# Decoder block on one core: order of the closing steps in the input projection (rotary tiles, squares, second half)

## The chip, the cores and the metric

One core of one Trainium2 chip. The metric is the time on the device in microseconds (us) for one execution of the whole kernel, the median of several runs. TensorE (PE) multiplies matrices, VectorE (DVE) and ScalarE (ACT) work on tiles of 128 partitions, GpSimd (POOL) does a few element-wise steps; SyncE (SP), ScalarE and GpSimd issue DMA transfers in their own instruction queues. Every engine works through its queue in order.

## The reference

All of it is float32; S = 1024 tokens, D = 1024. What bears on the change is the first sub-layer:

```python
h = _rmsnorm(x, g_mix_pre[l])                      # x * rsqrt(mean(x*x) + EPS) * g
proj = einsum('bsd,de->bse', h, w_in[l]) + b_in[l]
u_pool, q, k, v, gates = split(proj, IN_SPLITS)    # 512, 512, 128, 128, 2048
q = _partial_rotary(q.reshape(B, S, 8, 64), cos, sin)   # first 16 of 64 channels
k = _partial_rotary(k.reshape(B, S, 2, 64), cos, sin)
y_attn = _sliding_window_sink_attention(q, k, v, sinks) # window 128, blocks of 128
```

Behind it follow a pooling mixer, sigmoid gates that merge both branches, an output projection, and an MLP with a squared ReLU, each with an RMS norm and a residual sum.

## The kernel before

The work is laid out with channels on partitions and tokens along the free dimension. Each float32 product is made of three matmuls on rounded operands: a value is split into a high part (a cast, mostly on ScalarE) and a low part (a subtraction, on VectorE), and `PASSES` multiplies high by high, high by low and low by high.

**Projection.** `w_qkv` gives six tiles of 128 channels, f = 0 to 5; the tokens come in two halves, th = 0 and 1, of 512. Tiles 4 and 5 hold the rotary rows of all heads (80 rows: queries 0 to 3 in rows 16m, keys in rows 64 to 79) and the remaining key rows; tiles 0 to 3 hold the remaining query rows and, in rows 48 to 79, the values. `mm_in(f, th, k)` issues the three matmuls of one k of eight. `scaled(k, th, ...)` (L200 to L203) multiplies x by the norm's gain into the high part on ScalarE and the low part on VectorE. The norm's row factor comes later: `square_row` sums the squares of the tokens, `factors(th)` takes the inverse square root (`rsqrt`, L109 to L121) and spreads it (L218), and `make_rb(th)` transposes it with four matmuls on TensorE (L224) and copies it to `rb` (L225).

`close_in(f, th)` multiplies a finished tile by `rb` on VectorE (L350) and adds the bias on ScalarE (L351). `turn` (L360) and `turn_end` (L364, L365) rotate the rotary rows: for the first half on VectorE, for the second half on GpSimd. Then small DMAs put rows in place: `keys_rest` (L376, L377, two moves), `rows_in` (L372, three moves for the keys and three for each of the four query tiles), `values_out` (L380, one per query tile). `split_k` and `split_q(n)` make high and low parts for the scores.

**Order.** In the first block only TensorE's order is as written; a planner sets the order of the other engines by data and its own costs. In the second block (from L941) the order of TensorE, VectorE and ScalarE is the written one; SyncE's and GpSimd's queues are set by the planner. After the first half's tiles come the squares of the second half's tokens (L949), the closes of tiles 4 and 5, the turn, and the closes of tiles 0 to 3, each followed by its `rows_in` on SyncE, ScalarE, ScalarE and GpSimd.

**The stream.** `others()` is a generator that yields groups of three matmuls: first the 48 groups of the second half (tiles 4, 5, 0, 1, 2, 3, eight k each), then the gates' products (`half`). `fill(t)` takes groups from it until t us of TensorE time (0.681 us per group) are issued, carrying the rest over in `owed`. When the last k of a tile is issued, the tile is closed at that place in the queues of VectorE and ScalarE, with its moves in SyncE's queue. Between the fills lie the attention steps of the eight blocks n: scores (`score_all`, L439 to L441), masks (`score_prev`, L448), maximum (L455), exponentials (L465), scaling (L471), transposes (`attend_t`, L482), products with the values (`attend_v`, L507) and the transposes of the values (`post_v`, L403). The operands of the gates are prepared by callbacks in `between`, flushed inside `half`, or at f = 3, k = 3 for the first of them.

PSUM has four rotating banks with the tag `mm`, for the second half's tiles, `make_rb`, `post_v` and the gates. SBUF tiles of one tag rotate too: three of tag `st` hold weights that come from memory.

Of the kernel before, what the change touches and what calls it, by code (L numbers as in the profile page):

```python
# [17 lines left out]
NT = S // P  # L18
# [32 lines left out]
def block_kernel(ctx: ExitStack, tc, xt, x, consts, vecs, sinks, rot, g_post, g_mlp, g_mlp_post,  # L51
# [132 lines left out]
    def mm_in(f, th, k, a=0, b=512):  # L184

        for j, (wh, xh) in enumerate(PASSES):
            pe.matmul(b_in[f, th][:, a:b], w_in_of(f, k, wh), xs_[k][th][:, xh, a:b],  # L187
                      start=k == 0 and j == 0 and a == 0, stop=k == NK - 1 and j == 2)
# [11 lines left out]
    def scaled(k, th, xs, a=0, b=512):  # L200
        t, gk = xs_[k][th], vec[:, V_G + k:V_G + k + 1]
        act.activation(t[:, 0, a:b], xs[:, a:b], AF.Identity, scale=gk)
        dve.scalar_tensor_tensor(t[:, 1, a:b], xs[:, a:b], gk, f32(t[:, 0, a:b]), ALU.mult, ALU.subtract)  # L203
# [21 lines left out]
        act.copy(rb[:, th * 512:(th + 1) * 512], b)  # L225

    NR = 80
    squares_late, rows_of = {}, {}
    tables = {}

    def load_table(th):
# [3 lines left out]
    with tc.manual_schedule(engines={mybir.EngineType.PE}):  # L235
        for k in range(NK):
            if k % 2 == 0:
                xs = at("s4", 4, [S])
                wkv.append(ga_.tile([P, 2, 2, 256], F32R, tag="ga", name=nm("wkv")))
            xk = xs[:, k % 2 * 512:(k % 2 + 1) * 512]  # L240
            ws = stage([768]) if k else ws_first
            if k == 0:
                nc.sync.dma_start(vec, vecs)
                for a, b in ((0, 256), (256, 512)):
                    nc.sync.dma_start(xk[:, a:b], xt[k][:, a:b])
                nc.sync.dma_start(ws[:, 512:], w_qkv[k][:, 512:])
            else:
                nc.sync.dma_start(xk, xt[k][:, :512])
                nc.sync.dma_start(ws, w_qkv[k])
            xs_.append([xp.tile([P, 2, 512], F32R, tag="x", name=nm("x")) for _ in range(2)])  # L250
            q = wslot([2, 512]) if k < 6 else ga_.tile([P, 2, 512], F32R, tag="ga", name=nm("wq"))
            kv = wkv[-1]
            wq.append(q)
            if k == 0:
                split(q[:, 0, :], q[:, 1, :], ws[:, :512], first=dve)
                scaled(k, 0, xk, 0, 256)
                scaled(k, 0, xk, 256, 512)
            else:
                scaled(k, 0, xk)
                split(q[:, 0, :], q[:, 1, :], ws[:, :512])  # L260
            split(kv[:, 0, k % 2, :], kv[:, 1, k % 2, :], ws[:, 512:])
            if k == 0:
                for a in (0, 256):
                    for f in range(4):
                        mm_in(f, 0, k, a, a + 256)
            elif k < 6:
                for f in range(4):
                    mm_in(f, 0, k)
            if k < 6:
                for f in (4, 5):  # L270
                    mm_in(f, 0, k)
        for f in (4, 5, 0, 1):
            for k in (6, 7):
                mm_in(f, 0, k)
        nc.sync.dma_start(cst, consts)
        for n in range(4):
            square_row(n, at("qkv", 3, [S]) if n < 3 else at("s4", 4, [S]))
        load_table(0)
        factors(0)
        for k in range(NK):  # L280
            if k % 2 == 0:
                xs = flat(yy.tile([P, 2, 512], F32, tag="y", name=nm("xs")))
            nc.sync.dma_start(xs[:, k % 2 * 512:(k % 2 + 1) * 512], xt[k][:, 512:])
            scaled(k, 1, xs[:, k % 2 * 512:(k % 2 + 1) * 512])
        for n in range(4, NT):
            squares_late[n] = at("s8", 3, [2, 4, P]).rearrange("p a b k -> p (a b k)") if n < 7 else at("s4", 4, [S])
            nc.sync.dma_start(squares_late[n], x[n])
# [86 lines left out]
    def keys_rest(q, th):  # L374
        t = raw_k[th] = at("s4", 4, [2, 512])[:, 0, :]
        q.dma_start(t[:48], raw_r[th][NR:, 0, :])  # L376
        q.dma_start(t[NR:], raw_r[th][NR:, 1, :])  # L377
# [9 lines left out]
    def split_v(src, tag, bufs):  # L387

        t = at(tag, bufs, [6, HD], F32R)
        pool.memset(f32(t[:, ::5, :]), 0.0)  # L390
        split(t[:, 1::3, :], t[:, 2:4, :], src, pool, pool)
        return flat(t)
# [7 lines left out]
    def post_v(n):  # L400
        b = bank("mm")
        t = tv[:, n * P:(n + 1) * P]
        pe.transpose(b[:, :P], t, ident)  # L403
        act.copy(t, b[:, :P])
        vf, old = (tv[:, i * P:(i + 1) * P].rearrange("p (h d) -> p h d", d=HD) for i in (n, max(n - 1, 0)))
        vs[n] = split_v(vf, "v", 4)
        if n:
            dv = at("df", 1, [2, HD])
            pool.tensor_tensor(dv, vf, old, ALU.subtract)
            dvs[n] = split_v(dv, "dv", 3)  # L410

    scores = {}
    SCALE = HD ** -0.5
# [361 lines left out]
    def others():  # L775
        for f in (4, 5, 0, 1, 2, 3):
            b_in[f, 1] = bank("mm")
            for k in range(NK):
                mm_in(f, 1, k)
                if f == 3 and k == 3:  # L780
                    flush(between[0])
                    flush(between[1])
                if k == NK - 1:
                    close_in(f, 1)
                    if f == 5:
                        keys_rest(nc.sync, 1)
                        turn(1, pool)
                        turn_end(1, pool)
                        rows_in(nc.sync, 1, raw_k[1], 4)
                    elif f < 4:  # L790
                        values_out(nc.sync, 1, f)
                    if f in (1, 2, 3):
                        rows_in(nc.sync, 1, raw_of(f - 1, 1), f - 1)
                    if f == 1:
                        split_k(1)
                yield 3 * 0.227
            if f == 2:
                gt.load(2 * spilled[0])
                between[0].append(lambda: gt.operand(spilled[0], 1))
        gt.load(2 * spilled[1])  # L800
        steps = [(p, i) for p in spilled + (6, 7) for i in (1, 2)]
        for j, (p, i) in enumerate(steps[:16]):
            if j == 1:
                rows_in(nc.sync, 1, raw_of(3, 1), 3)
            if j == 0:
                between[0].append(lambda: gt.operand(*steps[1]))
                between[0].append(lambda: gt.operand(*steps[2]))
            between[0].append(lambda j=j: gt.operand(*steps[j + 3]))
            if i == 1:
                gt.load(2 * steps[j + 4][0])  # L810
            gi = 3 - j // 4
            if j in (0, 4, 9, 13):
                load_wb(gi)
            yield from half(p, i)
            if j % 4 == 3:
                flush(lazy)
                yield from wb_mm(gi)
# [125 lines left out]
    with tc.manual_schedule(engines={mybir.EngineType.PE, mybir.EngineType.DVE, mybir.EngineType.Activation}):  # L943
        make_rb(0)
        for f in (2, 3):
            for k in (6, 7):
                mm_in(f, 0, k)
        for n in range(4, NT):
            act.activation(squares_late[n], squares_late[n], AF.Square, accum_out=ssq[:, n:n + 1])  # L949
        close_in(4, 0)  # L950
        close_in(5, 0)
        turn(0, dve)
        keys_rest(nc.sync, 0)
        turn_end(0, dve)
        rows_in(nc.sync, 0, raw_k[0], 4)
        for m in range(4):
            close_in(m, 0)
            rows_in((nc.sync, nc.scalar, nc.scalar, nc.gpsimd)[m], 0, raw_of(m, 0), m)
        for m in range(4):
            values_out(nc.gpsimd, 0, m)  # L960
        load_table(1)
        factors(1)
        fill(4.0)
        make_rb(1)
        act.activation(warm, r1[:, :1], AF.Exp)
        fill(1.4)
        presum(0)
        presum(0)
        dve.tensor_scalar(nsnk, snk, -1.0, None, ALU.mult)
        split_k(0)  # L970
        fill(6.5)
        split_q(0)
        fill(1.6)
        score_all(0)
        act.activation(tv[:, :512], tv[:, :512], AF.Identity, bias=vec[:, V_BV:V_BV + 1])
        score_prev(0, 0)
# [22 lines left out]
        for n in range(NT):  # L999
# [5 lines left out]
            if n + 1 < NT:  # L1005
                early = 1.0 if n > 2 else 0.0
                softmax_exp(n + 1, range(4))
                fill(early)
                softmax_exp(n + 1, range(4, 8))
                softmax_scale(n + 1)  # L1010
                if n != 2:
                    flush(lazy)
                fill((5.0 if n == 1 else 4.4) - early)
                hurry[0] = True
                fill(1.4)
                hurry[0] = False
                if n + 2 < NT:
                    split_q(n + 2)
            else:
                fill(4.0)  # L1020
                split_gate(0, lambda: xp.tile([P, 2, 512], F32R, tag="x", name=nm("T")))
# [1486 lines left out]
```

## Time and profile before

| | |
|---|---|
| median of 3 runs | 1124.87 us (1122.95 to 1125.82) |
| the profiled execution's time | 1125.5 us |
| its span, first to last instruction | 1123.7 us |
| mean granted TensorE clock | 0.982 |
| instructions | 14805 |
| ScalarE busy | 647.4 us (58%) |
| GpSimd busy | 100.0 us (9%) |

The profile is one execution. Times in its views are microseconds from the first instruction. A group or timeline row names the line, the engine, the operation, the output and the inputs, the shape, the count and the duration; in brackets stands the idle time of the engine just ahead and what ended it. `PEld` is TensorE's weight load, which overlaps its matmuls; `ACTq` and `SPq` are the queues of ScalarE and SyncE issuing DMAs. The granted clock is the share of full speed that the throttle let TensorE have in a stretch. An L101 or L104 is the split into high and low part, wherever it is called from, so it is told apart by its tile (`qt` queries, `khi` and `klo` keys, `wh` weights).

### The profile page before, as it was taken

What the parts mean: (1) busy time and instruction counts of PE and PEld (TensorE: products, weight loads), DVE (VectorE), ACT (ScalarE), POOL (GpSimd) and SP (SyncE); (2) the same over time, 40 slices, a digit from 0 to 9 for tenths busy, and PEclk for the clock granted to TensorE, in tenths of its full rate; (3) what the DMA queues carried; (4) which work ended last, traced back from release to release, by engine and by line L of the source; (5) the groups of instructions that cost most, each with busy time, mean ns of one, the idle gap of its engine ahead of it and who ended that gap; (6) DMA issues with size and microseconds to landing.
All of it is one profiled execution on the core that took longest, in us unless ns stands there. A gap on an engine that the chain in (4) does not pass through costs nothing.

```text
span 1123.7 us, 14805 instructions
## 1 busy us (share of the span) xinstructions
PE 1086.7 (97%) x5247; PEld 908.9 (81%) x5247; DVE 904.2 (80%) x1300; ACT 647.4 (58%) x1084; POOL 100.0 (9%) x149
## 2 busy tenths in 40 slices
PE   9588899999999999999999999999999999999997
PEld 7466678788888888888888888888888899899886
DVE  5557599899978788778997967777665899889997
ACT  6536688746665425758676665655554375275553
POOL 0132143110010001200000000010100000000000
PEclk9879899999999999999999999999999999999999
DMA  8634677977986576763257755555698868549842
GB/s 290 225 90 123 198 188 186 313 232 247 307 246 217 172 231 167 171 241 131 71 177 284 272 199 215 197 192 202 237 397 291 270 221 288 169 146 317 310 155 75
DMA packets 107593, 243.29 MB, mean 217 GB/s; under 512 B 10656, under 2 KB 28320, under 8 KB 107520
## 3 DMA queue, kind: packets, MB, share of 16 engines
q1 hardware_dynamic: 87152, 192.48, 50.9%
q0 software_dynamic: 14336, 29.69, 11.0%
q10 hardware_dynamic: 6032, 20.19, 4.7%
q8 instruction: 41, 0.67, 0.2%
q14 instruction: 32, 0.26, 0.1%
HBM read 166.30 MB, written 73.40 MB: 213 GB/s over the span
## 4 chain that ended last, share of the span: by engine, by line
PE 84%; DVE 6%; ACT 4%; DMA 3%; issue 2%; ACTq 0%; SPq 0%; DVEq 0%
PE mm L626 24%; PE at L626 18%; PE at L2193 12%; PE mm L2193 5%; PE mm L1587 5%; PE at L2167 4%; PE mm L2167 4%; PE mm L537 3%; PE at L1587 2%; PE at L1315 2%; PE mm L187 1%; PE mm L1315 1%; PE mm L539 1%; ACT s L465 1%; PE sc L439 1%
## 5 line engine op out<-in xcount | busy, mean ns | idle before, releaser
L2193 PE MATMUL at<-ar,wh 128*128 128x512 f32 x564 | 134.6, 389 | 0.0
L2193 PEld LDWEIGHTS at<-ar,wh 128*128 128x128 f32 x564 | 105.8, 188 | 22.2 <-DVE ar L104 0.3
L104 DVE TENSOR_TENSOR wh<-st,wh 128x512 fp32r<-128x512 f32 (+1 forms) x106 | 77.9, 745 | 32.0 <-ACT wh L101 28.3
L101 ACT CAST wh<-raw 128x1024 fp32r<-128x1024 f32 (+1 forms) x54 | 53.4, 988 | 79.5 <-PE at L2193 52.0
L626 PE MATMUL mm<-T,wx 128*128 128x512 f32 x375 | 90.6, 389 | 0.0
L104 DVE TENSOR_TENSOR wh<-raw,wh 128x1024 fp32r<-128x1024 f32 (+1 forms) x54 | 61.7, 1143 | 29.7 <-ACT wh L101 29.2
L626 PEld LDWEIGHTS mm<-T,wx 128*128 128x128 f32 x375 | 70.3, 188 | 14.8 <-DVE wx L104 0.2
L101 ACT CAST wh<-st 128x512 fp32r<-128x512 f32 (+2 forms) x105 | 67.6, 653 | 19.7 <-DVE st L582 5.7
L626 PE MATMUL mm<-gr,wh 128*128 128x512 f32 x321 | 77.5, 391 | 0.0
L626 PEld LDWEIGHTS mm<-gr,wh 128*128 128x128 f32 x321 | 59.9, 188 | 12.2
L2193 PE MATMUL mm<-ar,wh 128*128 128x512 f32 x276 | 69.5, 389 | 0.0
L626 PE MATMUL mm<-T,wh 128*128 128x512 f32 x267 | 66.0, 389 | 0.0
L626 PE MATMUL mm<-x,wh 128*128 128x512 f32 x240 | 60.2, 401 | 3.9 <-ACT wh L101 3.9
L101 ACT CAST ar<-B 128x1024 fp32r<-128x1024 f32 (+2 forms) x59 | 43.0, 757 | 30.7 <-PE mm L2193 14.8
L2193 PEld LDWEIGHTS mm<-ar,wh 128*128 128x128 f32 x276 | 51.8, 188 | 10.8
L626 PE MATMUL at<-gr,wh 128*128 128x512 f32 x243 | 59.0, 389 | 0.0
L626 PEld LDWEIGHTS mm<-T,wh 128*128 128x128 f32 x267 | 50.1, 188 | 10.4
L626 PEld LDWEIGHTS mm<-x,wh 128*128 128x128 f32 x240 | 45.0, 191 | 14.1 <-ACT wh L101 4.4
L626 PEld LDWEIGHTS at<-gr,wh 128*128 128x128 f32 x243 | 45.6, 188 | 9.5
L626 PE MATMUL at<-T,wx 128*128 128x512 f32 x213 | 52.2, 389 | 0.0
L104 DVE TENSOR_TENSOR ar<-B,ar 128x1024 fp32r<-128x1024 f32 (+2 forms) x59 | 49.2, 857 | 1.1 <-ACT ar L101 1.1
L2167 PE MATMUL at<-ar,wh 128*128 128x256 f32 x336 | 47.5, 283 | 0.0
(560 smaller groups left out, 2491.2 us busy)
## 6 DMA issues: line engine op xcount, KB each, us to landing
raw<-f_dram SPq DMA_DIRECT2D x40, 512.0 KB, 4.6
B<-in_w_dn_dram SPq DMA_DIRECT2D x32, 512.0 KB, 8.2
st<-in_w_up_dram SPq DMA_DIRECT2D x27, 512.0 KB, 5.6
f_dram<-g SPq DMA_DIRECT2D x21, 512.0 KB, 3.3
wh<-f_dram SPq DMA_DIRECT2D x20, 512.0 KB, 5.9
g<-spill_dram SPq DMA_DIRECT2D x17, 512.0 KB, 5.9
st<-in_w_g_dram SPq DMA_DIRECT2D x16, 512.0 KB, 4.5
f_dram<-g ACTq DMA_DIRECT2D x16, 512.0 KB, 6.1
```

The lines of the kernel that those rows point to most:

```text
L101: act.copy(hi, src)
L104: return eng.tensor_tensor(lo, src, f32(hi), ALU.subtract)
L187: pe.matmul(b_in[f, th][:, a:b], w_in_of(f, k, wh), xs_[k][th][:, xh, a:b], start=k == 0 and j == 0 and a == 0, stop=k == NK - 1 and j == 2)
L439: pe.matmul(sb[:, kv, i, :nk], qt[r, qx, m * P:(m + 1) * P], kx[r, k0:k0 + nk], start=j == 0, stop=j == 2)
L465: act.activation(s8[:, h], s8[:, h], AF.Exp, scale=SCALE, bias=nmx[:, h:h + 1], accum_out=den[:, h:h + 1])
L537: pe.matmul(bs[th], whi[:, k, :], rhs(k, hl, th), start=k == 0 and hl == 0, stop=False)
L539: pe.matmul(bs[th], wlo[:, k, :], rhs(k, 0, th), start=False, stop=k == nk - 1)
L626: pe.matmul(b, w[wh][:, kt, :], x_, start=not after and kt == 0 and j == 0, stop=kt == 3 and j == 2, skip_group_check=after)
L1315: pe.matmul(b, w[wh][:, kt, :], xo[xh][:, kt, :], start=not after and kt == 0 and j == 0, stop=kt == 1 and j == 2, skip_group_check=after)
L1587: pe.matmul(bs[t], Am[a][k][ah][:, t * P:(t + 1) * P], Wm[w][k][wh], start=not after and k == 0 and j == 0, stop=k == 3 and j == 2, skip_g ...
L2167: pe.matmul(part[q][:, t, :], o[fs][fh][:, fk, t * P:(t + 1) * P], o[ws][wh][:, wk, :], start=q not in onto and (s_, t, j) == (0, 0, 0), s ...
L2193: pe.matmul(bs[t], fo[fh][:, k2, t * P:(t + 1) * P], wo_[wh][:, k2, :], start=not after and s2 == 0 and k2 == 0 and j == 0, stop=(s2, k2) ...
```

## The change

In the first block the scalings of the second half's x stop at k = 3; the other four go into the second block. There the order becomes: close of tiles 4 and 5, scaling of k = 4, turn, `keys_rest`, scaling of k = 5 to 7, `turn_end`, keys' `rows_in`, then the squares, the four closes of tiles 0 to 3, `factors(1)`, and only then the query tiles' row moves, two tiles' in SyncE's queue, one's in ScalarE's and one's in GpSimd's. The first fill takes 8.8 us in place of 4.0, the ones behind it less (13.6 in place of 13.5 us in all).

The close of a second-half tile is put off to k = 2 of the next tile, that is three groups later, once `make_rb(1)` has been issued (`ready`). All row moves of the second half go into GpSimd's queue in place of SyncE's. `split_k(1)` moves from the close of tile 1 to block n = 0's loop, `split_q(n + 2)` in that loop ahead of the fill (but for n = 2), and the first load of gate weights to the end of tile 1 instead of tile 2.

```diff
-            scaled(k, 1, xs[:, k % 2 * 512:(k % 2 + 1) * 512])
+            if k < 4:
+                scaled(k, 1, xs[:, k % 2 * 512:(k % 2 + 1) * 512])
+            else:
+                x_late.append((k, 1, xs[:, k % 2 * 512:(k % 2 + 1) * 512]))
...
+    closing, ready = [], [False]
+
+    def second_half(f):
+        close_in(f, 1)
+        if f == 5:
+            keys_rest(nc.gpsimd, 1)
+            turn(1, pool)
+            turn_end(1, pool)
+            rows_in(nc.gpsimd, 1, raw_k[1], 4)
+        elif f < 4:
+            values_out(nc.gpsimd, 1, f)
+        if f in (1, 2, 3):
+            rows_in(nc.gpsimd, 1, raw_of(f - 1, 1), f - 1)
...
                 mm_in(f, 1, k)
+                if k == 2 and ready[0]:
+                    flush(closing)
...
                 if k == NK - 1:
-                    close_in(f, 1)
-                    if f == 5:
-                        keys_rest(nc.sync, 1)
-                        turn(1, pool)
-                        turn_end(1, pool)
-                        rows_in(nc.sync, 1, raw_k[1], 4)
-                    elif f < 4:
-                        values_out(nc.sync, 1, f)
-                    if f in (1, 2, 3):
-                        rows_in(nc.sync, 1, raw_of(f - 1, 1), f - 1)
-                    if f == 1:
-                        split_k(1)
+                    closing.append(lambda f=f: second_half(f))
                 yield 3 * 0.227
-            if f == 2:
+            if f == 1:
                 gt.load(2 * spilled[0])
...
             if j == 1:
-                rows_in(nc.sync, 1, raw_of(3, 1), 3)
+                flush(closing)
+                rows_in(nc.gpsimd, 1, raw_of(3, 1), 3)
...
+        close_in(4, 0)
+        close_in(5, 0)
+        scaled(*x_late[0])
+        turn(0, dve)
+        keys_rest(nc.sync, 0)
+        for x_ in x_late[1:]:
+            scaled(*x_)
+        turn_end(0, dve)
+        rows_in(nc.sync, 0, raw_k[0], 4)
         for n in range(4, NT):
             act.activation(squares_late[n], squares_late[n], AF.Square, accum_out=ssq[:, n:n + 1])
-        close_in(4, 0)
-        close_in(5, 0)
-        turn(0, dve)
-        keys_rest(nc.sync, 0)
-        turn_end(0, dve)
-        rows_in(nc.sync, 0, raw_k[0], 4)
         for m in range(4):
             close_in(m, 0)
-            rows_in((nc.sync, nc.scalar, nc.scalar, nc.gpsimd)[m], 0, raw_of(m, 0), m)
+        factors(1)
+        for m, q in enumerate((nc.sync, nc.sync, nc.scalar, nc.gpsimd)):
+            rows_in(q, 0, raw_of(m, 0), m)
         for m in range(4):
             values_out(nc.gpsimd, 0, m)
         load_table(1)
-        factors(1)
-        fill(4.0)
+        fill(8.8)
         make_rb(1)
+        ready[0] = True
         act.activation(warm, r1[:, :1], AF.Exp)
-        fill(1.4)
+        flush(closing)
         presum(0)
         presum(0)
...
         split_k(0)
-        fill(6.5)
+        fill(3.4)
         split_q(0)
-        fill(1.6)
+        fill(1.4)
         score_all(0)
...
                 if n != 2:
                     flush(lazy)
+                    if n + 2 < NT:
+                        split_q(n + 2)
+                if n == 0:
+                    split_k(1)
                 fill((5.0 if n == 1 else 4.4) - early)
...
-                if n + 2 < NT:
-                    split_q(n + 2)
+                if n == 2:
+                    split_q(4)
```

More of the change, by code (lines that the diff above doesn't have):

```diff
@@ L227, in block_kernel @@
     NR = 80
-    squares_late, rows_of = {}, {}
+    x_late, squares_late, rows_of = [], {}, {}
     tables = {}
```

## The prediction, made before the result was known

> **What bounds the kernel now.** I read the page first, then the busy time by stage, then what TensorE waited for, then each engine's timeline between 30 and 120 us, where the waits are.
>
> ```profile
> span 1123.7 us, 14805 instructions
> ## 1 busy us (share of the span) xinstructions
> PE 1086.7 (97%) x5247; PEld 908.9 (81%) x5247; DVE 904.2 (80%) x1300; ACT 647.4 (58%) x1084; POOL 100.0 (9%) x149
> ```
>
> The busy time by stage (length, then busy time and instructions of each engine, granted TensorE clock, DMA share, GB/s):
>
> ```profile
> 36.00:140.00 104.00, 78.11 (x379) 61.52 (x379) 64.15 (x96) 53.04 (x140) 24.78 (x36) 0.82 0.50 143
> 140.00:1124.00 984.00, 973.56 (x4717) 818.60 (x4715) 821.30 (x1165) 569.81 (x901) 73.97 (x102) 1.00 0.68 221
> ```
>
> TensorE is the bound. After 140 us it idles 10.4 of 984 us at full clock, so whatever is won ahead of 140 us reaches the end. Between 36 and 140 us it idles 104 - 78.1 = 25.9 us at a granted clock of 0.82: this is the stage that the change edits. The longest waits of TensorE (total, times, longest):
>
> ```profile
> PE mm L224 <- DVE s L218: 13.8, 1, 13.8
> PE sc L439 <- DVE qt L104: 4.4, 4, 1.6
> PE mm L626 <- ACT wh L101: 3.9, 1, 3.9
> ```
>
> And where they lie in TensorE's timeline (start, duration, line, operation, count, idle before):
>
> ```profile
> 38.80 4.24 PE L187 MATMUL mm<-x,wkv 128*128 128x512 f32 x18
> 56.85 1.09 PE L224 MATMUL mm<-cst,s 128*128 128x128 f32 x4 [13.81 <-DVE s L218]
> 57.59 9.56 PE L187 MATMUL mm<-x,wkv 128*128 128x512 f32 x30
> ...
> 82.52 0.38 PE L439 MATMUL sc<-klo,qt 64*128 64x256 f32 x2
> ...
> 100.28 0.50 PE L439 MATMUL sc<-klo,qt 64*128 64x256 f32 x2 [2.29 <-ACT qt L101]
> ```
>
> Six groups of second-half matmuls (18) run at 4.24/18, about 0.23 us each; then the queue holds the four transposes of make_rb(1), and TensorE stands 13.8 us for the row factors of the second half. A wait also costs clock: the next 30 matmuls take 9.56 us instead of 30 x 0.23 = 6.9, so 2.7 us more. The same after the two smaller waits, by the granted clock (the number ahead of DMA share and GB/s):
>
> ```profile
> 76.00:78.00 2.00, 2.00 (x6) 1.52 (x6) 1.97 (x2) 1.08 (x3) 0.68 (x1) 0.50 0.08 16
> 78.00:80.00 2.00, 2.00 (x7) 1.56 (x6) 1.54 (x5) 0.00 (x0) 0.00 (x0) 0.52 0.09 16
> ...
> 100.00:102.00 2.00, 1.72 (x14) 1.47 (x16) 0.77 (x3) 1.96 (x4) 0.00 (x0) 0.60 0.14 33
> 102.00:104.00 2.00, 2.00 (x16) 1.74 (x15) 1.97 (x4) 1.09 (x2) 0.00 (x0) 0.55 0.58 110
> ```
>
> Four microseconds at 0.51 lose 2.0 us, four at 0.57 lose 1.7.
>
> **Part A: the second half's factors.** Why they come at 56.8 us is in ScalarE's timeline:
>
> ```profile
> 31.47 5.00 ACT L202 ACTIVATE x<-xs,vec 128x512 fp32r<-128x512 f32 x8
> 36.38 0.56 ACT L225 COPY rb_all<-mm 128x512 f32<-128x512 f32 x1
> 36.85 1.06 ACT L949 ACTIVATE s<-s 128x1024 f32<-128x1024 f32 x1
> ...
> 49.07 2.52 ACTq L372 DMA_DIRECT2D qkv<-qkv  x3
> 51.63 0.72 ACT L351 ACTIVATE qkv<-s,vec 128x512 f32<-128x512 f32 x1 [2.59 <-DMA qkv<-qkv]
> 52.38 1.90 ACTq L372 DMA_DIRECT2D qkv<-qkv  x3
> 54.33 0.72 ACT L351 ACTIVATE qkv<-s,vec 128x512 f32<-128x512 f32 x1 [1.98 <-DMA qkv<-qkv]
> 54.96 0.28 ACT L109 ACTIVATE sm<-ssq,eps 128x4 f32<-128x4 f32 x1
> ```
>
> The square root of factors(1) stands behind four biases, and between these ScalarE itself issues six row moves (2.52 + 1.90 us). VectorE's durations for the same stretch, and for two operations needed below:
>
> ```profile
> 32.96 5.39 DVE L203 SCALAR_TENSOR_TENSOR x<-xs,vec,x 128x512 fp32r<-128x512 f32 x8
> ...
> 43.38 2.36 DVE L360 TENSOR_TENSOR s<-qkv,s 80x1024 f32<-80x1024 f32 x2 [3.84 <-ACT qkv L351]
> ...
> 46.99 2.47 DVE L350 TENSOR_TENSOR s<-sc,rb_all 128x512 f32<-128x512 f32 x4
> ...
> 68.96 4.89 DVE L104 TENSOR_TENSOR qt<-qkv,qt 128x256 fp32r<-128x256 f32 x2 [1.09 <-ACT qt L101]
> 73.77 1.79 DVE L448 COPY_PREDICATED s<-cst,pad 128x512 f32<-128x512 uint32 x1
> ```
>
> I lay the new order on these. ScalarE scales k 0 to 3 until 34.0; the copy of rb still waits for TensorE (36.4 to 36.9). VectorE closes the two rotary tiles by 38.2 (2 x 0.62), ScalarE biases them by 39.0 and scales k=4 by 39.7. That adds a wait: VectorE's low part of k=4 (0.67 us) ends at 40.4; behind it stand the turn (2.36, to 42.7), the lows of k 5 to 7 (2.0, to 44.7) and turn_end (two of half width, about 1.25, to 46.0). The four closes follow to 48.4. ScalarE meanwhile has its scalings done at 41.5 and four squares (1.08 apart) at 45.9: the biases hide behind VectorE's closes, the last ends at 49.2, and the square root goes at 49.1 with no DMA issue ahead of it. From the square root to the transposes the row above takes 56.85 - 54.96 = 1.9 us: **transposes at 51.0**.
>
> TensorE runs 13 groups (39 matmuls, fill(8.8)) in place of 6 from 38.8. The low part of k=5 is due at 42.4 and comes at 43.4: a stall of 1.0 us that is new. Then it ends at 38.8 + 9.0 + 1.0 = 48.8 and waits 2.2 us. The gain is 56.85 - 51.0 = 5.85 us plus the 21 matmuls already done, 21 x 0.23 = 4.8: **10.6 us**. The slow stretch behind costs 2.7 us now; I keep it, because a wait of 2.29 us at 100.28 was enough for a clock of 0.60 and 0.55. Its bounds are 0 and 2.7, so up to 2.7 us more to win. [...]
>
> Costs at nothing: ScalarE's three moves for m=2 now follow the square root (49.4 to 51.9 with the dearer row) and the copy of rb waits for the transposes until 52.0; without that cover they cost up to 2.5. SyncE takes three more moves, some 1.9 us. The moves land in time:
>
> ```profile
> DMA to landing us min/median/max: 1.8/1.9/2.5
> ```
>
> SyncE's eleven moves, keys included, at 1.90/3 = 0.63 us each from 45, end near 52 and land by 54.5; the casts of split_q(0) are due near 55.5. Were SyncE's keys_rest held up by a buffer until the squares are through, it would be 1 us tighter.
>
> **Part B: first scores and the turn on GpSimd.** After the transposes (57.59 - 56.85 = 0.7 us) come 42 second-half matmuls before and 21 after, the first ones slow. They end near 51.0 + 0.7 + 21 x 0.23 + 2.7 = 59.2. Keys and queries are split by 58, since VectorE no longer waits there for TensorE to close a tile. So the waits of 1.3 and 1.6 us inside score_all(0) (2.9 of the 4.4 above) go, and with them the slow clock to 80 us (2.0 by the two rows shown, more by the time before them): 4.9 us.
>
> But what stretched the queries' lows to 2.45 us each was GpSimd:
>
> ```profile
> 68.72 4.85 POOL L360 TENSOR_TENSOR s<-qkv,s 80x1024 f32<-80x1024 f32 x2 [11.87 <-ACT qkv L351]
> 73.64 1.33 POOL L364 TENSOR_TENSOR qkv<-s,s 80x512 f32<-80x512 f32 x1
> ```
>
> VectorE's two lows begin and end with GpSimd's two products, and the masked copy at 73.77 took 1.79 beside the next one. The change doesn't remove that; it starts the turn after the bias of f=5, near 59, with two moves (taken at the same 0.63 us) ahead: 60.3 to 68. There VectorE has the two masked copies of block 0, the maximum and the lows of split_q(1). The two copies end after the two products, near 65.2; the maximum after 66.7; the lows near 68. TensorE reaches score_all(1) after nine groups of fill and the scores, near 66: a wait of 1 to 2 us, with some 2 us of clock behind. I take -3.5 (bounds 0 and -4.9), so B nets **+1.4 us**. [...]
>
> **Part C: split_q(2) and the close of f=2.** Now the queries of block 2 stand behind the close and bias of f=2, so TensorE waits 2.29 us at 100.28 and loses 1.7 to the clock. After, the cast follows the last exponential directly; the close, 0.6 on each engine, comes three groups later. What remains is the lows behind the softmax's scaling, some 1 us or none. split_k(1) comes after split_q(2) and isn't ahead of a score. 4.0 less 1.0: **+3.0** (bounds 0 and 4.0).
>
> **Part D: close of f=3 and gate operands.** The 3.9 us at L626 wait for a cast queued behind the close and bias of f=3. Both move behind it: VectorE's 0.62 and ScalarE's 0.72 go, and some more by the earlier row loads. The softmax scaling ahead stays. **+1.9** (bounds 0 and 3.9).
>
> Row moves of the second half: 21 issues leave SyncE, whose loads then stand behind fewer waits (0 to 1 us, taken as nothing); on GpSimd 21 x 0.6 = 13 us hide in its idle time (24.8 busy of 104).
>
> **Sum.** 10.6 + 1.4 + 3.0 + 1.9 = 16.9 us. The profiled execution took 1125.5 us, 1.8 around its span; 0.6 over the median of 1124.87. 1124.9 - 16.9 = **1108.0 us**. With every bound good: B +4.9, C 4.0, D 3.9, clock 2.7 give 26.1, or 1099. With B, C, D at their worst only A is left.
>
> **Rivals.**
> 1. *Only A holds.* The masks, softmax and splits on VectorE and ScalarE become the bound from 60 to 115 us and take B to D: 10.6 won, **1114.3**. For it: VectorE 64 of 104 us busy, and more per us once the stage shortens. Against: both engines sat waiting for TensorE and DMA there.
> 2. *GpSimd's turn doesn't hold TensorE,* because the fills cover it: 3.5 and some clock better, **1102 to 1104.5**. For it: GpSimd may start later or earlier than VectorE's copies. Against: both hang on the same bias.
> 3. *Slower: the second half's keys come too late through GpSimd.* Two moves, the turn (4.85 + 1.33 + about 1.7), three moves and a landing of 2.5 make 13 us from the bias near 59: 72 us. split_k(1) now stands in ScalarE's queue in block 0's loop, near 83, with the operands of the gates behind it. From 11 us of delay each further one costs one; past 28 it is slower than before, say **1130**. For it: GpSimd's queue is in order and VectorE can hold it. Against: those 11 us.
> 4. *No change:* the row factors come as late as before, because a load or the lows hold the chain: **1124**. Against: the eight scalings ran from 31.47 without a wait, so their data is there, and the lows are priced from rows.
>
> **Chances.** Forecast 1108 (1104.5 to 1111.5): 0.45. Rival 1 (to 1118): 0.25. Rival 2 (to 1099): 0.22. Rival 3: 0.04. Rival 4: 0.04. The range 1100 to 1116 leaves out some 2 in 10. 0.3% is 3.4 us, what a measurement here can tell: faster 0.92, same 0.04, slower 0.04.
>
> **What would show it.** Right: transposes of make_rb(1) near 51 with 2 to 3 us of wait; six-move gap on ScalarE gone; a clock near 0.5 to 57; first scores near 59; VectorE's masked copies of block 0 stretched to 2 us beside GpSimd's products; no wait at score_all(2). Wrong: the lows of k 5 to 7 holding TensorE more than 1 us, transposes after 54, a wait in split_k(1) on GpSimd's moves, or new waits from 66 to 115 that eat B to D.

## The result, and the profile after

| | before | after |
|---|---|---|
| median | 1124.87 us | 1108.53 us (1106.74 to 1108.81, 3 runs) |
| ratio to before, 95% interval | | 0.9853 [0.9827, 0.9879] |
| span of the profiled execution | 1123.7 us | 1106.7 us |
| mean granted TensorE clock | 0.982 | 0.992 |

The change makes the kernel 16.3 us faster; 1108.0 was forecast. A later measurement of the same kernel (experiment 11) gave 1108.68 and a ratio of 0.9865 [0.9849, 0.9882]; its profile, with the same span of 1106.7 us, is called the second profile below. One execution of experiment 10 was slow (1359.0 us at a clock of 0.749) and is left out, since only executions in the usual, fast state are compared.

The busy time by stage, in the same stretch as before:

```profile
36.00:140.00 104.00, 89.98 (x484) 70.23 (x483) 79.06 (x119) 68.90 (x184) 45.83 (x72) 0.95 0.61 174
140.00:1107.00 967.00, 957.68 (x4609) 805.54 (x4607) 803.42 (x1143) 555.52 (x862) 64.07 (x87) 1.00 0.67 221
```

From 36 to 140 us TensorE is busy 90.0 us in place of 78.1, with 105 more matmuls done; the rest of the kernel has kept its pace (9.3 us idle in 967). What TensorE still waits for, the four longest:

```profile
PE mm L780 <- ACT wh L765: 2.8, 1, 2.8
PE sc L499 <- DVE s L465: 1.9, 1, 1.9
PE mm L224 <- DVE s L218: 1.8, 1, 1.8
PE sc L456 <- DVE klo L104: 1.5, 1, 1.5
```

The 13.8 us at L224 have become 1.8; the 2.8 at L780, the first products with w_bp, were there before (L763). The two waits of 1.9 and 1.5 are new: at the transposes of block 1's probabilities, for the masks of block 2, and at block 0's scores, for the keys' low part. TensorE's timeline (line numbers are 17 or 18 higher than before from L439 on):

```profile
43.23 5.57 PE L187 MATMUL mm<-x,wkv 128*128 128x512 f32 x23 [0.71 <-DVE x L203]
50.62 0.66 PE L224 MATMUL mm<-cst,s 128*128 128x128 f32 x4 [1.82 <-DVE s L218]
51.03 2.33 PE L187 MATMUL mm<-x,wkv 128*128 128x512 f32 x9
53.20 2.88 PE L187 MATMUL mm<-x,wh 128*128 128x512 f32 x12
57.54 0.33 PE L456 MATMUL sc<-klo,qt 64*128 64x128 f32 x2 [1.46 <-DVE klo L104]
...
65.86 0.38 PE L456 MATMUL sc<-klo,qt 64*128 64x256 f32 x2
...
67.77 0.50 PE L456 MATMUL sc<-khi,qt 64*128 64x256 f32 x4 [0.45 <-DVE qt L104]
...
74.11 1.06 PE L499 MATMUL sc<-cst,s 128*128 128x128 f32 x8 [0.36 <-DVE s L488]
...
88.56 1.09 PE L499 MATMUL sc<-cst,s 128*128 128x128 f32 x8 [1.85 <-DVE s L465]
...
95.28 0.73 PE L643 MATMUL mm<-x,wh 128*128 128x512 f32 x2 [0.83 <-ACT wh L101]
97.19 1.20 PE L643 MATMUL mm<-x,wh 128*128 128x512 f32 x4 [1.17 <-DVE wh L104]
...
101.49 0.39 PE L456 MATMUL sc<-klo,qt 64*128 64x256 f32 x2
```

The same three later places before the change:

```profile
89.19 1.04 PE L482 MATMUL sc<-cst,s 128*128 128x128 f32 x8
...
104.72 1.09 PE L482 MATMUL sc<-cst,s 128*128 128x128 f32 x8
...
120.66 0.39 PE L439 MATMUL sc<-klo,qt 64*128 64x256 f32 x2
```

And the same places in the second profile of the changed kernel:

```profile
50.56 0.66 PE L224 MATMUL mm<-cst,s 128*128 128x128 f32 x4 [1.85 <-DVE s L218]
...
57.48 0.33 PE L456 MATMUL sc<-klo,qt 64*128 64x128 f32 x2 [1.47 <-DVE klo L104]
...
64.26 0.39 PE L456 MATMUL sc<-klo,qt 64*128 64x256 f32 x2
66.32 0.50 PE L456 MATMUL sc<-khi,qt 64*128 64x256 f32 x4 [1.67 <-DVE qt L104]
...
67.74 0.80 PE L456 MATMUL sc<-khi,qt 64*128 64x256 f32 x4 [0.34 <-DVE qt L104]
...
76.36 1.03 PE L499 MATMUL sc<-cst,s 128*128 128x128 f32 x8
...
90.77 1.85 PE L499 MATMUL sc<-cst,s 128*128 128x128 f32 x8 [1.84 <-DVE s L465]
...
104.46 0.38 PE L456 MATMUL sc<-klo,qt 64*128 64x256 f32 x2
```

With them the gain can be split by stage, on the clock of the profiles. The 21 matmuls that moved ahead of the transposes count 0.23 us each (4.83). "After" and "gain" are of the first profile, the two columns behind them of the second.

| stage | before | after | gain | second profile | its gain | forecast |
|---|---|---|---|---|---|---|
| up to the transposes of make_rb(1) | 56.85 | 50.62 | 6.23 + 4.83 = 11.1 | 50.56 | 11.1 | 10.6 (A) |
| from there to block 0's transposes | 32.34 | 23.49 | 8.85 - 4.83 = 4.0 | 25.80 | 1.7 | 1.4 (B) |
| to block 1's transposes | 15.53 | 14.45 | 1.1 | 14.41 | 1.1 | 3.0 (C) |
| to the scores of block 3 | 15.94 | 12.93 | 3.0 | 13.69 | 2.2 | 1.9 (D) |
| from there to the end of the span | 1003.04 | 1005.21 | -2.2 | 1002.24 | 0.8 | 0 |
| sum | | | 17.0 | | 17.0 | 16.9 |

The sum met the forecast nearly to the tenth in both profiles. In the first the terms did not: B and D brought 3.7 us more, C and the rest 4.1 less. In the second A, B and D lie within 0.5 us of the forecast, C is 1.9 too small, and 0.8 comes from the rest. It is the same kernel in the same time: where TensorE's clock falls differs between the two (0.75 and 0.50 from 58 to 62 us in the first, 0.50 from 68 to 72 us in the second), and a stage differs by up to 3.0 us between them. A difference of that size in one stage of one profile says little by itself.

### The profile page after: what moved, and what is told of

It reads as the page before. It is cut to its first block, busy times and chain, and to the rows that moved or that the text cites. A ratio compares the mean times of both kernels' runs of the same rounds, so it can differ in the third digit from the quotient of the medians.

```text
span 1106.7 us, 14808 instructions
## 1 busy us (share of the span) xinstructions
PE 1082.6 (98%) x5247; PEld 904.6 (82%) x5247; DVE 901.2 (81%) x1300; ACT 647.1 (58%) x1084; POOL 111.2 (10%) x170
## 4 chain that ended last, share of the span: by engine, by line
PE 82%; DVE 5%; ACT 3%; issue 2%; DMA 1%; POOL 0%; DVEq 0%; SPq 0%; ACTq 0%
PE mm L643 24%; PE at L643 16%; PE at L2211 12%; PE mm L2211 5%; PE mm L1605 5%; PE at L2185 4%; PE mm L2185 4%; PE mm L554 3%; PE at L1605 2%; PE at L1333 2%; PE mm L1333 1%; PE mm L556 1%; PE sc L524 1%; DVE s L508 1%; ACT s L482 1%
## 5 line engine op out<-in xcount | busy, mean ns | idle before, releaser
L2211 PEld LDWEIGHTS mm<-ar,wh 128*128 128x128 f32 x276 | 51.8, 188 | 10.7
```

The source lines that it names most:

```text
L2211: pe.matmul(bs[t], fo[fh][:, k2, t * P:(t + 1) * P], wo_[wh][:, k2, :], start=not after and s2 == 0 and k2 == 0 and j == 0, stop=(s2, k2) ...
```

## The experiments

All times are medians; each ratio is to the kernel before, run on the same chip. A difference from the changed kernel is one of medians, and where the intervals of the two ratios overlap, the text says so.

**1. Everything but part A** (e1_old_order): all scalings in the first block, the old order of squares, closes and row moves, `factors(1)` last, fills 4.0, 1.4, 6.5, 1.6.

```diff
...
-        for m in range(4):
-            close_in(m, 0)
-        factors(1)
-        for m, q in enumerate((nc.sync, nc.sync, nc.scalar, nc.gpsimd)):
-            rows_in(q, 0, raw_of(m, 0), m)
+        for m in range(4):
+            close_in(m, 0)
+            rows_in((nc.sync, nc.scalar, nc.scalar, nc.gpsimd)[m], 0, raw_of(m, 0), m)
...
+        factors(1)
-        fill(8.8)
+        fill(4.0)
...
```

> Everything of the change but part A: the late squares ahead of the closes, all eight scalings in the first block, row moves between the closes, factors(1) last, the fills 4.0, 1.4, 6.5, 1.6. My theory (A is about two thirds of the gain): the transposes of make_rb(1) come at 56 to 57 us again and TensorE waits 13 to 14 us there; 10.6 us are lost and some 2 us of clock behind, so 1119 to 1122 us. Rival (A is all of it, the rest hides nothing): 1124 to 1126. Rival (the later parts catch up what A loses): 1112 to 1115.

1120.76 us, ratio 0.9958 [0.9944, 0.9973]. The transposes are at 57.15 again:

```profile
57.15 1.09 PE L224 MATMUL mm<-cst,s 128*128 128x128 f32 x4 [13.95 <-DVE s L218]
```

So A is worth 12.2 us on top of the rest, and the rest alone 4.2. As expected.

**2. Part A split** (e2_squares_first): squares and all scalings first again, row moves still behind `factors(1)`.

```diff
...
+        for n in range(4, NT):
+            act.activation(squares_late[n], squares_late[n], AF.Square, accum_out=ssq[:, n:n + 1])
         close_in(4, 0)
         close_in(5, 0)
-        scaled(*x_late[0])
         turn(0, dve)
         keys_rest(nc.sync, 0)
-        for x_ in x_late[1:]:
-            scaled(*x_)
         turn_end(0, dve)
         rows_in(nc.sync, 0, raw_k[0], 4)
-        for n in range(4, NT):
-            act.activation(squares_late[n], squares_late[n], AF.Square, accum_out=ssq[:, n:n + 1])
```

> Part A split: only the order of squares, scalings and closes is undone (squares first, all scalings in the first block); factors(1) stays ahead of the query tiles' row moves, the fills stay. My theory: most of A is ScalarE's six row moves; biases end near 50.3, transposes near 52.2, a wait near 4 us with a half clock behind it: 2 to 4 us over the changed kernel, 1110.5 to 1112.5. Rival (the order of squares and closes is what counts): transposes after 55, 1116 or more.

1111.26 us, ratio 0.9892 [0.9864, 0.9921]. The transposes are at 51.33, 0.7 us later than in the changed kernel, with a wait of 3.0 us ahead of them in place of 1.8. By the medians, some 9.5 of A's 12.2 us are the row moves taken from between ScalarE's biases, with the fills that go with them, and closes and scalings ahead of the squares bring about 2.7. The intervals of this kernel and the changed one overlap, so the second part is not told from nothing.

**3. Closes at once** (e3_close_at_once): the delay of three groups undone, all else kept.

```diff
-                if k == 2 and ready[0]:
-                    flush(closing)
...
                     closing.append(lambda f=f: second_half(f))
+                    if ready[0]:
+                        flush(closing)
```

> The second half's tiles are closed at their last k again (once make_rb(1) is issued), all else as in the change. My theory: the delay of three groups only spares VectorE's and ScalarE's waits for TensorE, and part D's 1.9 us: 1109 to 1111.5. Rival (the delay is worth nothing): 1108 to 1109. Rival (the delay costs, since GpSimd's turn starts later): 1106 to 1107.5.

1119.24 us, ratio 0.9952 [0.9937, 0.9968]: a miss by 8 us. Without the delay 10.7 us are lost. TensorE's timeline of this kernel at block 0's scores, then VectorE's and GpSimd's beside it:

```profile
58.97 0.47 PE L456 MATMUL sc<-klo,qt 64*128 64x128 f32 x2 [2.97 <-ACT qt L101]
...
64.54 0.69 PE L456 MATMUL sc<-khi,qt 64*128 64x128 f32 x4 [3.58 <-DVE qt L104]
```

```profile
58.95 5.54 DVE L104 TENSOR_TENSOR qt<-qkv,qt 128x256 fp32r<-128x256 f32 x2 [1.08 <-ACT qt L101]
```

```profile
59.53 4.67 POOL L363 TENSOR_TENSOR s<-qkv,s 80x1024 f32<-80x1024 f32 x2
```

Closed at once, tile 5 comes ahead of the queries' split in both queues: ScalarE casts the queries only after the tile's bias, and GpSimd's turn starts in time to hold VectorE over the queries' two lows (5.54 us; in the changed kernel 0.75). Block 0's scores wait 6.6 us, and the clock falls (0.73, then 0.50 from 58 to 62 us). By stage the loss has two places: up to block 0's transposes 28.7 us, in place of 23.5 and 25.8 in the two profiles of the changed kernel, and from block 1's transposes to block 3's scores 17.4 in place of 12.9 and 13.7, where TensorE waits 2.60 us for a gate operand, and where block 1's transposes with the nine matmuls behind them take 5.27 us in place of 3.02.

**4. Row moves in SyncE's queue** (e4_sync_queue): `nc.sync` for `nc.gpsimd` in `second_half` and in `others`.

> The second half's row moves go into SyncE's queue again, all else as in the change. My theory (taken as nothing in the prediction): within 1 us of the changed kernel, 1107.5 to 1109.5. Rival (SyncE's waits hold back loads of weights and sums): 1111 or more, with a longer wait of TensorE for a gate operand or for the first products with w_bp.

1110.89 us, ratio 0.9882 [0.9865, 0.9898]: 2.4 us slower and above my range, though the intervals overlap. GpSimd, rid of the key moves (the second stands right ahead of its turn in the changed kernel, at 59.71), starts the turn 1.0 us earlier:

```profile
59.31 5.22 POOL L363 TENSOR_TENSOR s<-qkv,s 80x1024 f32<-80x1024 f32 x2 [8.81 <-ACT qkv L354]
```

```profile
59.73 5.38 DVE L465 COPY_PREDICATED s<-cst,pad 128x512 f32<-128x512 uint32 x2 [1.26 <-ACT s L458]
```

Now both masks of block 0 fall wholly on GpSimd's products, and score_all(1) waits 3.6 us. The same two groups in the changed kernel:

```profile
60.33 5.37 POOL L363 TENSOR_TENSOR s<-qkv,s 80x1024 f32<-80x1024 f32 x2
```

```profile
59.93 3.54 DVE L465 COPY_PREDICATED s<-cst,pad 128x512 f32<-128x512 uint32 x2 [1.26 <-ACT s L458]
```

There the first mask begins before GpSimd does. Against the first profile this is where the time goes: 25.7 us to block 0's transposes in place of 23.5. But the second profile has 25.8 there too, with the turn at the same place as in the first. Against it this kernel loses its time later, at the gate operands: TensorE waits 0.83 and 1.80 us there in place of 1.33, and the stage to block 3's scores takes 14.9 us in place of 13.7. A longer wait for a gate operand is what the rival said. Which of the two costs the 2.4 us, if they are not noise, stays open.

**5. Splits late again** (e5_split_late).

```diff
                 if n != 2:
                     flush(lazy)
-                    if n + 2 < NT:
-                        split_q(n + 2)
-                if n == 0:
-                    split_k(1)
...
-                if n == 2:
-                    split_q(4)
+                if n + 2 < NT:
+                    split_q(n + 2)
+                if n == 0:
+                    split_k(1)
```

> split_q(n + 2) and split_k(1) go back behind the fills of block n's loop, all else as in the change. The prediction's part C: up to 3.0 us lost, with a wait of TensorE for block 2's queries near 2 us at score_all(2) and a half clock behind it: 1110 to 1112. Rival (the delayed close alone gives what C won, since nothing stands ahead of the cast any more): 1108 to 1109.

1109.62 us, ratio 0.9869 [0.985, 0.9888]: 1.1 us slower, between the two ranges, and its interval overlaps that of the changed kernel. Its profile has 0.42 us of wait at score_all(2), not 2, but 3.53 in place of 1.85 at block 1's transposes: the moved splits now stand later in VectorE's queue, ahead of block 2's masks. That stage takes 16.0 us, 1.6 more than in either profile of the changed kernel. The 0.42 us are for a copy of block 0's output. Block 2's queries hold TensorE up by some 0.2 us there, so the delayed close alone takes that wait away.

**6. Sums later** (e6_presum_later): `presum(0)` twice behind `split_q(1)`.

> The four sums of presum(0) on VectorE (2.8 us) go from ahead of split_k(0) to behind split_q(1). My theory: they are the new wait at the first scores (1.46 us for klo), and with it the half clock from 59 to 62.5 us (some 1.8 us) goes: 1105.5 to 1107. Rival (GpSimd's turn or the masks of block 1 behind the moved sums take it back): 1108 to 1109.5.

1112.82 us, ratio 0.9889 [0.9874, 0.9904]: 4.3 us slower, with intervals that just overlap; the rival's direction, and more than it said. The keys' low part is no earlier (57.3 us). VectorE idles 4.7 us ahead of tile 4's close, until the first half's row moves have landed:

```profile
55.35 0.69 DVE L353 TENSOR_TENSOR qkv<-mm,rb_all 128x512 f32<-128x512 f32 x1 [4.68 <-DMA qkv<-qkv]
```

In the changed kernel this idle time is 2.7 us: the close writes a `qkv` tile, and with three buffers of that tag it has to wait for moves out of an older one. Why it waits 2 us longer here is left open. The moved sums stand ahead of block 1's masks, and TensorE waits 4.5 us for block 0's scaling.

**7. A longer wait** (e7_wait_longer): fills 7.5 and 4.7 for 8.8 and 3.4.

> Two groups of three matmuls go from ahead of make_rb(1) to behind it (fill 7.5 and 4.7 in place of 8.8 and 3.4); nothing else. TensorE's wait for the row factors grows from 1.8 to about 3.2 us. Prediction's theory (a wait of over 2 us costs the clock): half clock behind the transposes, the first scores reached near 60 us without a wait: 1109 to 1111. Rival (the clock holds through a wait of this length as it does through 1.8 us): the two groups fill the wait at the first scores, 1107 to 1108.5.

1108.32 us, ratio 0.9858 [0.9843, 0.9873]: no change. The wait grew to 2.55 us and the clock did fall behind it:

```profile
52.00:54.00 2.00, 2.00 (x7) 1.54 (x6) 0.92 (x2) 1.35 (x3) 0.00 (x0) 0.50 0.48 162
```

But then TensorE reached block 0's scores at 58.07 without a wait, and the clock stayed up there (1.00 from 56 to 66 us). In this profile and the first of the changed kernel the clock is lost once between 50 and 66 us, behind the one wait (0.50 and 0.70 from 52 to 56 us) or behind the other (0.75, 0.50 and 0.89 from 58 to 64 us).

**8. No turn for the second half** (e8_no_turn): its four operations are left out, and the rotary rows are moved unrotated.

> The second half's turn on GpSimd (four products and sums) is left out: the rotary rows of the second half are moved unrotated. My theory: GpSimd's reading holds VectorE (the two masks 3.54 us, the two lows of split_q(1) 1.84 us); without it these take 1.4 and 0.8, but TensorE waits only 1.0 us there, so 1106.5 to 1108. The prediction's size for it (3.5 us of wait and clock): 1104.5 to 1105.5. Rival (no hold, other reasons): 1108 to 1109 with the masks still near 3 us.

1106.06 us, ratio 0.9838 [0.982, 0.9855]. The masks take their own time, and score_all(1) has no wait:

```profile
59.80 1.36 DVE L464 COPY_PREDICATED s<-cst,pad 128x512 f32<-128x512 uint32 x2 [1.26 <-ACT s L457]
```

By the medians the hold costs the changed kernel 2.5 us, but the intervals overlap, and the four executions lie near 1104.5 (two) and 1107.6 (two). Up to block 0's transposes this kernel takes 22.0 us, 1.5 less than the changed kernel's first profile and 3.9 less than its second. It lost the clock behind the keys' wait of 1.48 us, as the first did (the next six matmuls of the second half took 2.93 us in both, 1.65 in experiment 12), so 1.5 is the fairer of the two.

**9. Sums first, close of tile 4 later** (e10_sums_first).

```diff
-        flush(closing)
         presum(0)
         presum(0)
         dve.tensor_scalar(nsnk, snk, -1.0, None, ALU.mult)
         split_k(0)
         fill(3.4)
         split_q(0)
+        flush(closing)
         fill(1.4)
```

> The changed kernel, with the first closes of the second half (tile 4) put behind split_q(0) instead of ahead of presum(0): VectorE's sums of presum(0) then fill its idle 2.7 us before the first half's row moves have landed, and keys and queries of block 0 no longer stand behind them. My theory: the wait of 1.46 us at the first scores goes and with it the half clock from 59 to 62.5 us: 1105 to 1106.5, with scores near 56.2 us. Rival (GpSimd's turn then falls on other operations of VectorE and takes it back): 1108 to 1109. Rival (the sums' inputs or the row moves come late): 1109 or more, first scores after 58.

1109.78 us, ratio 0.9872 [0.9848, 0.9897]: no gain. The wait at block 0's scores is gone (the keys' low ends at 54.5), but the turn now starts at 58.1, ahead of both masks, and they take 7.57 us beside GpSimd's operations:

```profile
59.06 7.57 DVE L465 COPY_PREDICATED s<-cst,pad 128x512 f32<-128x512 uint32 x2 [2.65 <-ACT s L458]
```

TensorE waits 4.1 us in score_all(1), and the stage to block 0's transposes takes 26.2 us, no less than in the changed kernel. The rival named this mechanism; its range ended 0.8 us lower.

**10. Part A alone** (e11_only_a): e3 with the moves in SyncE's queue and the splits and first gate load at their old places.

> Part A alone: its order, row moves and fills; the second half's tiles closed at their last k, moves in SyncE's queue, split_q, split_k(1) and the first gate load at their old places. The prediction's rival 1 gave A alone 1114.3 us, if what A wins is kept. My theory now: without the delayed close the queries' lows of block 0 fall on GpSimd's turn and wait for tile 5's bias on ScalarE, which takes half of A back: 1118 to 1121, with 5 us or more of waits in the first scores. Rival (the waits are due to the change's other parts): 1112 to 1115.

1116.04 us (1115.61 to 1116.67), ratio 0.9936 [0.9912, 0.9961], between the two ranges, with 4.5 us of waits in the first scores. A alone wins 8.4 us; the rest alone won 4.2 (experiment 1); together they win 15.8 (experiment 11) or 16.3. Some 3 to 4 us seem to be won only by both, but by the good ends of the two intervals (9.9 and 6.3 us) none of it need be.

**11. The changed kernel again** (e12_after_again), beside e10 and e11.

> The changed kernel itself, on the same chip as e10, to set the two side by side: 1108.5 us, within 0.2%.

1108.68 us, ratio 0.9865 [0.9849, 0.9882]: the time of the first measurement. Its profile is the second one above.

**12. e10 with the turn on VectorE** (e13_turn_vector).

```diff
         if f == 5:
             keys_rest(nc.gpsimd, 1)
-            turn(1, pool)
-            turn_end(1, pool)
-            rows_in(nc.gpsimd, 1, raw_k[1], 4)
+            turn(1, dve)
...
         split_q(1)
+        turn_end(1, dve)
+        rows_in(nc.gpsimd, 1, raw_k[1], 4)
```

> e10 with the second half's turn on VectorE: its two products behind tile 5's close, its two sums behind split_q(1), the keys' row moves behind those; nothing is left out. My theory: what GpSimd's turn costs is VectorE held for its whole length (e10: two masks 7.57 us, 4.1 us of wait in score_all(1)); on VectorE the turn takes 3.7 us, of which some 2.6 fall into its idle time ahead of the masks, the two masks take 1.4 us, and score_all(1) waits under 0.5 us: 1104 to 1106. Rival (VectorE is the bound there, so its 3.7 us come back as waits): 1107.5 to 1109, with waits at score_all(1) or at the first transposes of the probabilities.

1104.77 us (1103.27 to 1104.85), ratio 0.9825 [0.981, 0.984]: faster than both kernels, its interval clear of that of the repeated changed kernel (it touches that of the first measurement).

```profile
57.14 2.36 DVE L363 TENSOR_TENSOR s<-qkv,s 80x1024 f32<-80x1024 f32 x2 [0.81 <-ACT qkv L354]
59.42 1.36 DVE L463 COPY_PREDICATED s<-cst,pad 128x512 f32<-128x512 uint32 x2
```

The turn fills VectorE's idle time ahead of the masks, these run unheld, and neither block 0's nor block 1's scores wait. The stage to block 0's transposes takes 20.3 us. Of the 5.0 us between this and e10, some 1.6 are the clock behind the transposes, which stayed up here (1.00 from 52 to 56 us) and fell there (0.50, 0.65) after a wait of the same 1.8 us.

## Why the prediction was right, and where it was not

**Part A: right, in place and size.** Transposes forecast at 51.0, measured 50.62 and 50.56; the new stall forecast at 1.0, measured 0.71; the wait forecast at 2.2, measured 1.82. ScalarE's timeline shows the step: biases in one run and the square root right behind, with one move issued before it.

```profile
46.34 2.56 ACT L354 ACTIVATE qkv<-s,vec 128x512 f32<-128x512 f32 x4 [0.88 <-DVE s L353]
48.33 0.61 ACTq L375 DMA_DIRECT2D qkv<-qkv  x1
48.81 0.28 ACT L109 ACTIVATE sm<-ssq,eps 128x4 f32<-128x4 f32 x1
```

Experiments 1 and 2 show the moves, with the fills, to be the larger half. What A wins isn't kept by itself: alone it is 8.4, not 10.6.

**The clock behind the transposes: mis-sized.** I kept 2.7 us of loss. The 21 matmuls from 51.03 take 5.05 us at a clock of 1.00 (50 to 56 us), so the loss went. It came back later. In the first profile it came behind the next wait, the 1.46 us at block 0's scores (0.75, then 0.50):

```profile
58.00:60.00 2.00, 2.00 (x24) 1.79 (x23) 0.74 (x3) 1.30 (x3) 0.29 (x1) 0.75 0.76 258
60.00:62.00 2.00, 2.00 (x7) 1.51 (x6) 2.00 (x2) 1.60 (x4) 1.90 (x2) 0.50 0.45 102
```

In the second profile the clock stayed up there and fell behind the waits within score_all(1):

```profile
58.00:60.00 2.00, 2.00 (x26) 1.80 (x25) 0.73 (x3) 1.36 (x3) 0.35 (x1) 1.00 0.71 241
...
68.00:70.00 2.00, 2.00 (x12) 1.69 (x13) 0.74 (x2) 1.68 (x4) 2.00 (x4) 0.50 0.06 11
70.00:72.00 2.00, 2.00 (x6) 1.47 (x6) 0.93 (x3) 2.00 (x12) 1.26 (x3) 0.50 0.24 50
```

In the two profiles of the changed kernel the clock stayed up behind a wait of 1.82 and 1.85 us for the row factors. But 2.55 us in experiment 7 were enough to lose it (0.50 from 52 to 54 us), and so were 1.85 in experiment 9 (0.50, then 0.65 from 52 to 56 us).

**Part B: the mechanism right; how near its size came depends on the profile.** GpSimd's turn did hold VectorE: the masks took 3.54 and 3.61 us in the two profiles, the two lows of split_q(1) 1.84 and 1.83, and without the turn 2.5 us are won by the medians (experiment 8; I had put 3.5). I had forecast 1 to 2 us of wait within score_all(1) and 2 of clock behind it. In the second profile that came as forecast: 1.67 and 0.34 us of wait, the clock at half behind them, and a stage gain of 1.7 for my 1.4. In the first profile TensorE, slowed behind block 0's scores, came there 1.6 us later and waited only 0.45 us, and the clock stayed up (1.00 from 64 to 76 us). Seven groups, not the nine I wrote, lie between the two scores; the time near 66 us goes with seven. Missed in both was the wait of 1.46 us for the keys, whose low stands behind 2.8 us of sums, and these behind a close that waits 2.69 us for landed moves.

I also said that the waits in score_all(0) go because VectorE no longer waits for TensorE to close a tile. Experiment 3 shows the larger reason: the late close puts GpSimd's turn behind the queries' lows (60.33 behind 57.31; closed at once, 59.53 beside lows from 58.95). In the sum I had not seen how much hangs on that. Closed at once, nothing of B would have come: 28.7 us there, and before, without the 21 matmuls, 27.5.

**Part C: too large.** 3.0 forecast, 1.1 by stage in both profiles. The wait for the queries went, and either the delayed close (experiment 5) or the earlier splits (experiment 3, where 0.36 us are left) is enough for that. What the sum put at nothing are the waits that come next: 0.92 us for a copy of block 0's output and 1.85 for block 2's masks, behind presum(1) on VectorE. What the earlier splits bring is 1.1 us by the medians of experiment 5, within its noise, and 1.6 by stage.

**Part D: right.** The wait at the gate operands is 0.83 + 1.17 = 2.0 us in place of 3.94, the 1.9 forecast; the further 1.1 us in that stage I put down to the clock, 0.51 and 0.63 from 114 to 118 us before and 1.00 from 90 to 104 us after. In the second profile the wait is 1.33 us and the stage gains 2.2. With the closes at once the wait is 2.60 us (experiment 3), and 3.96 with A alone (experiment 10). So the moved close shortens it by 0.6 to 1.3 us, and the other moves that experiment 3 keeps, the earlier gate load among them, by 1.4; which of them does it was not tested. The stage is some 4 us longer in both (17.4 and 17.0). In experiment 3 some 2.3 us of this are the slower transposes and matmuls (5.27 us in place of 3.02), in experiment 10 2.0 are the longer wait; what the remainder is was not shown.

**The rest: not foreseen, and in part chance.** In the first profile 2.2 us are given back behind block 3's scores, in the second 0.8 are won. About 1.1 of the 2.2 is at the first products with w_bp, where TensorE waits 2.80 and then 1.11 us, the second time for VectorE's low part:

```profile
112.67 0.73 PE L780 MATMUL mm<-wh,wpt 128*128 128x512 f32 x2 [2.80 <-ACT wh L765]
114.51 2.07 PE L780 MATMUL mm<-wh,wpt 128*128 128x512 f32 x4 [1.11 <-DVE wh L768]
```

In the second profile the second wait is 0.89 us. The other 1.2 is clock near 182 us, which the second profile does not lose (last section).

**Row moves off SyncE, taken as nothing:** 2.4 us by the medians, with intervals that overlap and the cause open (experiment 4).

**The rivals.** 1, that only A holds, is out: the rest adds 7.4 us to A (experiments 10 and 11). 2, that the turn's hold costs TensorE nothing, is out as well by the wait of 2.0 us within score_all(1) in the second profile. 3, late keys, did not come: `split_k(1)`'s cast runs at 79.96 without a wait. The total was right because the mechanisms of A, B and D were. That it came to within 0.5 us is luck: what C fell short by, A, B, D and the rest brought on top, and by the first profile misses of 4 us of either sign cancelled.

## What to carry to other kernels

An in-order engine that both computes and issues DMAs is a serial chain: put what others wait for ahead of the issues (here six of them, 4.4 us, stood ahead of a square root). Before delaying or advancing a step, look at what runs on the neighbouring engine at the new time; here a turn moved from GpSimd into VectorE's idle time made its stage 5.9 us shorter (26.2 us in experiment 9, 20.3 in 12, with 1.6 of it the clock behind the transposes), and that kernel beat both others. A forecast sum that comes true is no proof of its terms: compare stage by stage, and take a second profile of the same kernel before explaining a stage that is off by 2 or 3 us.

## What the runs showed that was not expected

In these runs the length of a short wait alone did not decide whether the clock fell behind it. At the transposes the wait was 1.82 to 1.87 us in ten profiles. Behind it the clock stayed at 1.00 in seven (both of the changed kernel, experiments 3, 5, 6, 8 and 12) and fell to 0.50 in three (experiments 4, 9 and 10, where the next nine matmuls took 3.61, 3.30 and 3.67 us; 2.33 in the first profile of the changed kernel). At block 0's scores the changed kernel lost it behind 1.46 us in the first profile and kept it behind 1.47 in the second. And near 182 us the kernels before and after have the same three waits, 0.53, 0.49 and 0.34 us, but the 48 matmuls behind them ran at full speed before and partly at half in the first profile after (0.50 from 182 to 184 us, then 0.67):

```profile
201.24 11.05 PE L626 MATMUL mm<-x,wh 128*128 128x512 f32 x48
```

```profile
182.80 12.27 PE L643 MATMUL mm<-x,wh 128*128 128x512 f32 x48
```

In the second profile, behind waits of 0.52, 0.49 and 0.34 us, they ran at full speed again:

```profile
184.19 11.07 PE L643 MATMUL mm<-x,wh 128*128 128x512 f32 x48
```

So these 1.2 us are none of the change's. What else decides whether the clock falls, no run here shows.
